# Values token-major with 512 weight columns at once, the last 16 tokens in float32 on four column groups, and gates inside the attention heads

## The chip, the cores and the metric

The kernel runs on one core of one Trainium2 chip. The metric is the device time of one execution in microseconds (us); three runs of the kernel before gave 1594.56 to 1595.37 us with a median of 1594.84 us. One of its executions was taken by the hardware profiler, and every row below comes from that one. PE is the matrix engine, PEld its loading of the operand that stays in the array, ACT, DVE and POOL are the scalar, vector and general engines, SP issues most of the transfers.

## The reference

The reference is one transformer layer in float32 over 512 tokens with 16 learned tokens ahead of them (T = 528), width 1024: a gated feed-forward block, a mixer, a second feed-forward block and a last norm. Only the mixer matters here:

```python
proj = u @ w_in                       # u = rmsnorm(h); columns are split into
# rq rk (4 heads x 256), rv rg (4 x 512), aq ak av (8 x 128), iq ik iw, g_ret, g_att
yr = retention(rope(rq), rope(rk), rv)    # 4 heads, values 512 wide
yr = (silu(rg) * yr) @ w_ret_out
ya = dsa_attention(rope(aq), rope(ak), av, rope(iq), rope(ik), iw) @ w_att_out
merged = sigmoid(g_ret) * yr + sigmoid(g_att) * ya
return merged @ w_mix_out
```

In both branches a weight matrix over pairs of tokens (decayed q·k in retention, a softmax over selected keys in attention) is multiplied with the values `rv` or `av`. The keys that attention selects come from an index score, made from `iq`, `ik` and `iw`, of which the 128 best per token are kept.

## The kernel before

Activations lie with features on the 128 partitions and tokens along the free dimension. Every float32 factor is split into two parts of the type fp32r: `hi` is a rounded copy made by ACT (L117), `lo` the rest made by DVE (L118). `mm3` (L152) then makes three matmuls for each of the 8 blocks of 128 input features: hi·hi, lo·hi, hi·lo. A weight tile of 128 output columns is the stationary operand and the tokens stream past it, 512 of them in one matmul, or all 528 in two of 264. So one projection of 128 columns is 24 matmuls of 512 or 48 of 264 columns. Weights come by transfers of up to 1 MB into two buffers (`raw`), and their split parts go into three buffers each (`whi`, `wlo`).

The order of PE's instructions is the order of the program text (PE is under `manual_schedule`). The other engines' instructions are put in order by a scheduler that works by dependencies and program order. Background work, the index scores (`index_steps`) and the choice of the keys (`select_steps`), is cut into steps that the program calls for between projections with `step()`.

The mixer goes like this:

1. Index projections: `psiq` four times, `psik` once; then rotary embedding on ACT, DVE and POOL, which yields `iw` (L593), `ikh` (L599) and `ikl` (L600), the operands of the index scores `psw` (L606) and `pssc` (L617). The scores' two matmuls of a pair use 64 rows of the array each.
2. Retention, four heads. For each head: query (`psrq`, twice) and key (`psrk`, twice), each pair turned by `rope_pair` (DVE L688, POOL L691, then the split into `rkh` and `rkl`); the output projection of the head before (`ret_out`, `psro`); then four blocks of 128 value columns. For each block stand: `gated()`, the gate's projection `psrg`; `values()`, the value projection `psrv` over all 528 tokens; in the first block `decayed()`, the decayed scores `psst` (L751); `weigh()` of the block before, `pspv` (L771, tail L772); and `by_token()`, in which PE turns the block's values so that tokens lie on the partitions: four transposes of 128x128 (L788) and one for the last 16 tokens (L789), whose results ACT and DVE split. In the first head the gate and the value projection of the first block stand between the key projection and `decayed()`, and index steps are held back until the key projection.
3. Attention, eight heads: `psaq`, `psak`, `psav`, scores `psS` (L936), softmax, transposes of the probabilities `psPT` (L952), `psao` (L771), and the same `by_token()` (L788, L789). While one head's softmax runs, PE makes the next head's projections. Six of the eight `g_ret` gates (`psgate`) come in the last head and after it.
4. After the heads: the eight `g_att` gates (`psga`), the output projection of attention (`psat`), the last projection of the mixer (`psmo`).

The second feed-forward block's down projection (`psd`, L1143) already has the other layout: 128 tokens of the hidden activations are stationary, and 512 columns of weights stream, four blocks of tokens for each piece of weights of four feature blocks.

Of the kernel before, what the change touches and what calls it, by code (L numbers as in the profile page):

```python
# [18 lines left out]
P = 128  # L19
D = 1024  # L20
# [61 lines left out]
def kernel(ctx: ExitStack, tc: tile.TileContext, x, meta, g1, wg1, wu1, wd1, gm,  # L82
# [113 lines left out]

    def rstd_steps(ssum, n, dim, dst, sp, psum):


        ends = [min(b * P, n - P) for b in range(-(-n // P))]  # L200
        nb = len(ends)
        col = psum()
        for b, t0 in enumerate(ends):
            nc.tensor.matmul(col[:, b : b + 1], ssum[:, t0 : t0 + P], ones, start=True, stop=True)
        yield from rstd_of(col, n, dim, dst, sp, psum, P - (n - S))

    def rstd_of(col, n, dim, dst, sp, psum, tail):
# [4 lines left out]
        r = sp.tile([P, 5], F32, tag="rcol", name="rcol", bufs=2)  # L212
# [39 lines left out]

    gap(cpool, 8)


    with pool("f1") as fp, pool("gps", 2, PSUM) as gps, ExitStack() as later:
# [205 lines left out]
        for f0, nf in ((0, 12), (12, 10)):  # L462
# [38 lines left out]
            for c in range(0, KD, 2):  # L501
# [7 lines left out]
                for i in range(2):  # L509
                    k = c + i  # L510
                    nc.vector.scalar_tensor_tensor(hT[k], halves(pss[i])[1], 0.5, hT[k], ALU.mult, ALU.add)
                    if f0:
                        h, l = new_x(k, XO)
                        split_gain(hT[k], gains[:, 1, k : k + 1], h, l)
                        add_square(hT[k], ssum2, k == 0, fp, bufs=4)
                        nc.scalar.dma_start(hd[k], hT[k][:, REAL])
# [48 lines left out]
    with pool("ixt") as ixt:  # L565
        tp.update(pool=ixt, bufs=8)
        norm = rstd_steps(ssum2, T, D, R2, ixt, lambda: mm_tile("psn"))
        pss = []
        cols = Cols(w_in, OFF_IQ, 4)
        for i in range(4):  # L570
# [4 lines left out]
            if i < 3:  # L575
                next(norm)
        cos, sin = rope_tables(0, ixt)
        iq = []
# [68 lines left out]
    def tails(p, n):  # L647

        tp.update(v=[stacked(p, f"vtail{i}", P) for i in range(2)], p=stacked(p, "ptail", n), turn=0)

# [26 lines left out]
    with pool("rt") as rt:  # L677
        tp.update(pool=rt, bufs=7)
        cos, sin = rope_tables(2, rt)
        gap(rt, 48)  # L680
# [84 lines left out]
        def weighted(ps, vb, prob):  # L765

            for kb in range(4):
                vh, vl = vb[0][:, kb, :], vb[1][:, kb, :]
                ph, pl = prob[kb]
                for i, (a, b) in enumerate(((vh, ph), (vh, pl), (vl, ph))):  # L770
                    nc.tensor.matmul(ps[:, KQ[kb] :], a, b, start=kb == 0 and i == 0, stop=False)  # L771
            nc.tensor.matmul(ps[:, KQ[4] :], vb[2][:TR], tp["p"][:TR, :NM], start=False, stop=True)  # L772

        def weigh(c, vb, sg, prob, ssum, o):
# [4 lines left out]
            nc.vector.tensor_tensor(t[:, :S], ps, sg, ALU.mult)  # L779
            oh = rt.tile([P, S], F32R, tag=f"oh{c}", name="oh")  # L780
            ol = rt.tile([P, S], F32R, tag=f"ol{c}", name="ol")
            split(t[:, :S], oh, ol)
            o.append((oh, ol))

        def by_token(vt, vp):
            ps = mm_tile("psvt").rearrange("p (a b) -> p a b", a=2)
            for kb in range(4):
                nc.tensor.transpose(ps[:, 0, kb * P : (kb + 1) * P], vt[:, kb * P : (kb + 1) * P], ident)  # L788
            nc.tensor.transpose(ps[:NM, 1, 0:P], vt[:, 4 * P : T], ident)  # L789
            vh = vp.tile([P, 4, P], F32R, tag="vh", name="vh", bufs=2)  # L790
            vl = vp.tile([P, 4, P], F32R, tag="vl", name="vl", bufs=2)
            split(ps[:, 0, :].rearrange("p (b c) -> p b c", b=4), vh, vl)
            tail = tp["v"][tp["turn"]]
            tp["turn"] ^= 1
            split_rows(ps[:NM, 1, 0:P], tail, "hhl")
            return vh, vl, tail

        bg = [index_steps()]
        last_weigh = last_norm = last_out = None
        for h in range(RH + 1):  # L800
# [20 lines left out]
            cols = Cols(w_in, OFF_RK + h * DK, 2)  # L821
            if h == 0:
                bg[0] = steps
            ka = proj_all(cols, "psrk")
# [13 lines left out]
            ssum = rt.tile([P, S], F32, tag="ossum", name="ossum", bufs=2)  # L838
            cv = Cols(w_in, OFF_RV + h * DV, 4)
            cg = Cols(w_in, OFF_RG + h * DV, 4)  # L840
# [9 lines left out]

            def values():
                ps = proj_all(cv, "psrv")
                vt = tmp()
                ins = nc.vector.tensor_tensor(vt, ps, R, ALU.mult)
                step(ins)
                return vt

            for c in range(4):
                if c == 0:
                    sg = gated()  # L860
                    vt = values()
                    prob = decayed(rq, rk, u)
                else:
                    vt = values()
                    sg = gated()
                    weigh(*pend, prob, ssum, o)
                if h == 0:
                    step()
                    step()
                pend = (c, by_token(vt, rt), sg)  # L870
            rn = rt.tile([P, S], F32, tag="rn", name="rn")
# [7 lines left out]


    with pool("ao") as ao:
        ao_parts = []
        with pool("at") as at:
# [10 lines left out]
            tails(at, 48)  # L894
            cq, ck, cv = (Cols(w_in, o_, AH, step=1) for o_ in (OFF_AQ, OFF_AK, OFF_AV))
            scale = DH**-0.5
# [18 lines left out]

            def proj_v():
                w = cv.next()
                parts, ps = halves(mm_tile("psav"))
                mm3(parts, w, xs, KD)
                vt = tmp()  # L920
                nc.vector.tensor_tensor(vt, ps, R, ALU.mult)
                return vt

# [38 lines left out]

            def weigh_v(parts, v):
                ps = sm_tile("psao")
                weighted(ps, v, parts)
                oh = ao.tile([P, S], F32R, tag=f"ah{len(ao_parts)}", name="ah")
                ol = ao.tile([P, S], F32R, tag=f"al{len(ao_parts)}", name="al")
                split(ps, oh, ol)
                ao_parts.append((oh, ol))

            q, k, vt = proj_q(), proj_k(), proj_v()
            for h in range(AH):
                more = h + 1 < AH
                scores(q, k)
                if h == 0:
                    v = by_token(vt, at)
                if more:
                    q, k = proj_q(), proj_k()
                else:
                    for c in (2, 3, 4):  # L980
                        gate_acc(c, gate(gr, at, wide=True))
                parts = transpose_p()
                if more:
                    vt = proj_v()
                else:
                    gate_acc(5, gate(gr, at, wide=True))
                weigh_v(parts, v)
                if more:
                    v = by_token(vt, at)

# [4 lines left out]
        with pool("ou") as ou:  # L995
            tp.update(pool=ou, bufs=3)
            for c in (6, 7):
                gate_acc(c, gate(gr, ou))
            cols = Cols(w_in, OFF_GA, KD)
            sa = []  # L1000
            for c in range(KD):
                w = cols.next()
                ps = sm_tile("psga")
                mm3([(ps, REAL)], w, xs, KD)
                t = ou.tile([P, S], F32, tag=f"sa{c}", name="sa")
                nc.vector.tensor_tensor(t, ps, Rr, ALU.mult)
                nc.scalar.activation(t, t, AF.Sigmoid)
                sa.append(t)
            cols = Cols(w_ao, 0, KD)
# [14 lines left out]
    with pool("om") as ou:  # L1024
# [36 lines left out]
        for _ in norm:  # L1061
            pass
    mgs.close()
    accs.close()
    sel.close()
# [116 lines left out]
```

## Time and profile before

| quantity | value |
|---|---|
| median of three runs | 1594.84 us (1594.56 to 1595.37) |
| profiled execution | 1595.39 us |
| its span (first to last instruction) | 1593.5 us |
| PE busy | 1582.4 us in 9731 matmul records |
| DVE busy | 820.9 us |
| ACT busy | 570.6 us |
| POOL busy | 232.7 us |

The page's first part gives the busy time of each engine, the second the busy tenths in 40 slices of the span, the fourth the chain of work that ended last. In the timeline view each row has the start, the length, the engine, the line, the operation, what it writes and reads, and how many instructions of the same kind are merged in it; a row of PE begins with the shape of the stationary operand (rows*columns). Matmuls overlap, so their lengths don't add up: what one costs is the distance from its start to the next start.

### The profile page before, as it was taken

What the parts mean: (1) busy time and instruction counts of PE and PEld (TensorE: products, weight loads), DVE (VectorE), ACT (ScalarE), POOL (GpSimd) and SP (SyncE); (2) the same over time, 40 slices, a digit from 0 to 9 for tenths busy, and PEclk for the clock granted to TensorE, in tenths of its full rate; (3) what the DMA queues carried; (4) which work ended last, traced back from release to release, by engine and by line L of the source; (5) the groups of instructions that cost most, each with busy time, mean ns of one, the idle gap of its engine ahead of it and who ended that gap; (6) DMA issues with size and microseconds to landing.
All of it is one profiled execution on the core that took longest, in us unless ns stands there. A gap on an engine that the chain in (4) does not pass through costs nothing.

```text
span 1593.5 us, 23010 instructions
## 1 busy us (share of the span) xinstructions
PE 1582.4 (99%) x9731; PEld 1421.5 (89%) x9731; DVE 820.9 (52%) x1263; ACT 570.6 (36%) x912; POOL 232.7 (15%) x187
## 2 busy tenths in 40 slices
PE   9999999999999999999999999999999999999998
PEld 8999999999888898899898999988888888888886
DVE  5443234334575776866845666753454434324434
ACT  6322222233544333233333555553234323223223
POOL 1211001111320200301304210011002111001100
PEclk9999999999999999999999999999999999999999
DMA  5222232224332132231312322313243322232222
GB/s 185 90 84 83 93 113 80 97 80 143 108 112 67 42 116 78 80 116 40 119 54 72 112 69 66 94 58 103 80 138 101 118 96 89 89 113 90 93 91 81
DMA packets 148582, 148.66 MB, mean 93 GB/s; under 512 B 3288, under 2 KB 137456, under 8 KB 148480
## 3 DMA queue, kind: packets, MB, share of 16 engines
q1 hardware_dynamic: 143872, 138.16, 26.9%
q10 hardware_dynamic: 4544, 9.03, 1.7%
q8 instruction: 76, 1.25, 0.3%
q14 instruction: 26, 0.21, 0.0%
q0 software_dynamic: 64, 0.01, 0.0%
HBM read 143.00 MB, written 4.19 MB: 92 GB/s over the span
## 4 chain that ended last, share of the span: by engine, by line
PE 91%; DVE 4%; ACT 2%; issue 1%; POOL 1%; DMA 1%; ACTq 0%; POOLq 0%; DVEq 0%
PE psu L152 15%; PE psg L152 15%; PE psd L152 8%; PE psd L1143 7%; PE psrv L152 6%; PE psrg L152 6%; PE psrk L152 3%; PE psgate L152 3%; PE psmo L152 3%; PE psat L152 3%; PE psga L152 3%; PE psak L152 3%; PE psav L152 3%; PE psrq L152 2%; PE psro L152 2%; PE psaq L152 2%
## 5 line engine op out<-in xcount | busy, mean ns | idle before, releaser
L117 ACT ACTIVATE whi<-raw 128x1024 fp32r<-128x1024 f32 (+3 forms) x284 | 277.7, 979 | 841.8 <-PE psu L152 165.6
L118 DVE TENSOR_TENSOR wlo<-raw,whi 128x1024 fp32r<-128x1024 f32 (+3 forms) x284 | 338.6, 1192 | 179.0 <-ACT whi L117 175.3
L152 PE MATMUL psu<-xl,whi 128*128 128x264 f32 (+1 forms) x528 | 141.0, 319 | 0.0
L152 PE MATMUL psu<-xh,whi 128*128 128x264 f32 (+1 forms) x528 | 140.6, 318 | 0.0
L152 PE MATMUL psu<-xh,wlo 128*128 128x264 f32 (+1 forms) x528 | 140.6, 318 | 0.0
L152 PE MATMUL psg<-xl,whi 128*128 128x264 f32 (+1 forms) x496 | 133.3, 321 | 0.0
L152 PE MATMUL psg<-xh,wlo 128*128 128x264 f32 (+1 forms) x496 | 132.8, 321 | 0.0
L152 PE MATMUL psg<-xh,whi 128*128 128x264 f32 (+1 forms) x496 | 132.8, 320 | 0.0
L152 PEld LDWEIGHTS psu<-xh,wlo 128*128 128x128 f32 x528 | 88.1, 188 | 6.9
L152 PEld LDWEIGHTS psu<-xh,whi 128*128 128x128 f32 x528 | 87.8, 188 | 6.8
L152 PEld LDWEIGHTS psu<-xl,whi 128*128 128x128 f32 x528 | 87.4, 188 | 6.9
L152 PEld LDWEIGHTS psg<-xh,wlo 128*128 128x128 f32 x496 | 82.6, 188 | 6.9
L152 PEld LDWEIGHTS psg<-xh,whi 128*128 128x128 f32 x496 | 82.3, 188 | 6.7
L152 PEld LDWEIGHTS psg<-xl,whi 128*128 128x128 f32 x496 | 82.0, 188 | 6.8
L483 POOL TENSOR_TENSOR t<-t,R 128x528 f32<-128x528 f32 x22 | 37.5, 1707 | 262.3 <-ACT t L482 262.3
L1118 POOL TENSOR_TENSOR t<-t,R 128x512 f32<-128x512 f32 x22 | 38.4, 1748 | 251.6 <-ACT t L1117 251.6
L152 PE MATMUL psd<-hl,whi 128*128 128x264 f32 x352 | 71.3, 284 | 0.0
L152 PE MATMUL psd<-hh,wlo 128*128 128x264 f32 x352 | 70.8, 283 | 0.0
L152 PE MATMUL psd<-hh,whi 128*128 128x264 f32 x352 | 70.6, 282 | 0.0
L1143 PE MATMUL psd<-whi,hh 128*128 128x512 f32 x176 | 68.5, 389 | 0.0
L1143 PE MATMUL psd<-wlo,hh 128*128 128x512 f32 x176 | 68.5, 389 | 0.0
L1143 PE MATMUL psd<-whi,hl 128*128 128x512 f32 x176 | 68.5, 389 | 0.0
(316 smaller groups left out, 3555.8 us busy)
## 6 DMA issues: line engine op xcount, KB each, us to landing
raw<-in_w_in_dram SPq DMA_DIRECT2D x34, 1024.0 KB, 4.9
raw<-in_ffn_w_up_dram SPq DMA_DIRECT2D x22, 1024.0 KB, 5.0
raw<-in_ffn_w_gate_dram SPq DMA_DIRECT2D x21, 1024.0 KB, 5.0
raw<-in_w_in_dram SPq DMA_DIRECT2D x25, 512.0 KB, 3.5
raw<-in_ffn_w_down_dram SPq DMA_DIRECT2D x10, 1024.0 KB, 4.8
raw<-in_w_ret_out_dram SPq DMA_DIRECT2D x16, 512.0 KB, 3.4
raw<-in_ffn_w_down_dram SPq DMA_DIRECT2D x8, 768.0 KB, 4.3
raw<-in_ffn_w_down_dram SPq DMA_DIRECT2D x8, 640.0 KB, 3.9
```

The lines of the kernel that those rows point to most:

```text
L117: nc.scalar.activation(hi, src, AF.Copy)
L118: eng.tensor_tensor(lo, src, hi.bitcast(F32), ALU.subtract)
L152: nc.tensor.matmul(o, a[:, k, :], b[:, sl], start=first and k == 0 and i == 0, stop=last and k == nk - 1 and i == 2)
L483: nc.gpsimd.tensor_tensor(t, t, R, ALU.mult)
L1118: nc.gpsimd.tensor_tensor(t, t, R, ALU.mult)
L1143: nc.tensor.matmul(pss[b], a[:, bs], m[:, k % 2, :], start=k0 + k == 0 and i == 0, stop=k0 + k == nf - 1 and i == 2)
```

## The change

The values are now made token-major. `values(c0, parts, meanwhile)` takes 512 columns of weights in two pieces of four feature blocks (1 MB each). For each of four blocks of 128 tokens the tokens' activations are stationary and the 512 weight columns stream, so that the result already has tokens on the partitions; `split_gain` scales it by the token's norm factor (kept per token in `rtok`) and splits it. The five transposes of every block of 128 columns and their multiply are gone. One call replaces four `values()` and `by_token()` of a retention head, or of four attention heads: six calls in all. The last 16 tokens don't fill a block; they are multiplied in plain float32 out of the unsplit weights, with the activations of 16 tokens (`xlast`, scaled by POOL) stationary, 128 weight columns streaming, and the four groups of 128 weight columns written to partitions 0, 32, 64 and 96 of one PSUM tile `psvl`. `place()` splits those rows into four tiles `vtail`.

The order changes with it. In the first retention head `values` stands before the query projection and calls a background step after each block of tokens; the index steps are no longer held back. In the later heads it stands after `ret_out`. `decayed()` follows directly after it (in the first head: directly after the key projection), and the four gates follow, each but the first with a `weigh()` behind it. In attention two calls (before the first head's scores, and in the fourth head) replace `proj_v` of each head; in its place in the other heads stands one gate: six of `g_ret`, and in the last head three of `g_att`.

```diff
+    def values(c0, parts, meanwhile=lambda: None):
+        two = [mm_tile("psv") for _ in range(2)]
+        ps = [two[b // 2][:, b % 2 * S : (b % 2 + 1) * S] for b in range(4)]
+        rest = sm_tile("psvl")
+        for k0 in (0, 4):
+            raw = load_w(w_in[k0 * P : (k0 + 4) * P, c0 : c0 + 4 * P], 4, 4 * P)
+            w_at[0] = XO
+            ws = [split_w(raw[:, i : i + 2, :]) for i in (0, 2)]
+            w_at[0] = 0
+            for k in range(k0, k0 + 4):
+                for c in range(4):
+                    nc.tensor.matmul(rest[32 * c : 32 * c + NM, :P], xlast[:, k, :], raw[:, k - k0, c * P : (c + 1) * P],
+                                     start=k == 0, stop=k == KD - 1)
+            for b in range(4):
+                bs = slice(b * P, (b + 1) * P)
+                for k in range(4):
+                    (xh, xl), (wh, wl) = xs(k0 + k), ws[k // 2]
+                    for i, (a, m) in enumerate(((xh, wh), (xl, wh), (xh, wl))):
+                        nc.tensor.matmul(ps[b], a[:, bs], m[:, k % 2, :], start=k0 + k == 0 and i == 0,
+                                         stop=k0 + k == KD - 1 and i == 2)
+                if k0:
+                    split_gain(ps[b].rearrange("p (c d) -> p c d", c=4), rtok[:, b : b + 1],
+                               parts[0][:, :, bs], parts[1][:, :, bs])
+                meanwhile()
...
-        def by_token(vt, vp):
-            ps = mm_tile("psvt").rearrange("p (a b) -> p a b", a=2)
-            for kb in range(4):
-                nc.tensor.transpose(ps[:, 0, kb * P : (kb + 1) * P], vt[:, kb * P : (kb + 1) * P], ident)
-            nc.tensor.transpose(ps[:NM, 1, 0:P], vt[:, 4 * P : T], ident)
...
+            if h == 0:
+                place = values(OFF_RV, parts, step)
             cols = Cols(w_in, OFF_RQ + h * DK, 2)
-            if h == 0:
-                steps, bg[0] = bg[0], iter(())
...
+            if h:
+                place = values(OFF_RV + h * DV, parts, step)
+            prob = decayed(rq, rk, u)
+            vs = place()
...
             for c in range(4):
-                if c == 0:
-                    sg = gated()
-                    vt = values()
-                    prob = decayed(rq, rk, u)
-                else:
-                    vt = values()
-                    sg = gated()
+                sg = gated()
+                if c:
                     weigh(*pend, prob, ssum, o)
...
-                parts = transpose_p()
-                if more:
-                    vt = proj_v()
+                pt = transpose_p()
+                if h == 3:
+                    place = half_values(1)
+                elif more:
+                    wide_gate()
                 else:
-                    gate_acc(5, gate(gr, at, wide=True))
-                weigh_v(parts, v)
-                if more:
-                    v = by_token(vt, at)
+                    wide_gate_a()
+                weigh_v(h, pt, vs[h])
+                if h == 3:
+                    vs += place()
```

More of the change, by code (lines that the diff above doesn't have):

```diff
@@ L566 @@
         tp.update(pool=ixt, bufs=8)
-        norm = rstd_steps(ssum2, T, D, R2, ixt, lambda: mm_tile("psn"))
+        norm = rstd_steps(ssum2, T, D, R2, ixt, lambda: mm_tile("psn"), rtok)
         pss = []
@@ L647, in tails, with place @@
     def tails(p, n):
-        tp.update(v=[stacked(p, f"vtail{i}", P) for i in range(2)], p=stacked(p, "ptail", n), turn=0)
+        tp.update(v=[stacked(p, f"vtail{i}", P) for i in range(4)], p=stacked(p, "ptail", n))
+    def values(c0, parts, meanwhile=lambda: None):
[22 more added lines that the diff above has]
+                meanwhile()
+        def place():
+            for c in range(4):
+                rows = slice(32 * c, 32 * c + NM)
+                split_rows(rest[rows, :P], tp["v"][c], "hhl")
+            return [(parts[0][:, c, :], parts[1][:, c, :], tp["v"][c][:TR]) for c in range(4)]
+        return place
     def split_rows(src, t, order):
@@ L678 @@
         tp.update(pool=rt, bufs=7)
+        parts = [rt.tile([P, 4, S], F32R, tag=f"vo{i}", name="vo") for i in range(2)]
         cos, sin = rope_tables(2, rt)
@@ L767, in weighted @@
             for kb in range(4):
-                vh, vl = vb[0][:, kb, :], vb[1][:, kb, :]
+                vh, vl = (part[:, kb * P : (kb + 1) * P] for part in vb[:2])
                 ph, pl = prob[kb]
@@ L878, with gate_a @@
             gate_acc(c, t)
+    sas = ExitStack()
+    sap = sas.enter_context(pool("sap", 1, side="right"))
+    gr = Cols(w_in, OFF_GR + 2 * P, KD - 2, step=1)
+    ga = Cols(w_in, OFF_GA, KD, step=1)
+    sa = []
+    def gate_a(ps, gp):
+        mm3([(ps, REAL)], ga.next(), xs, KD)
+        t = gp.tile([P, S], F32, tag=f"sa{len(sa)}", name="sa")
+        nc.vector.tensor_tensor(t, ps, Rr, ALU.mult)
+        nc.scalar.activation(t, t, AF.Sigmoid)
+        sa.append(t)
     with pool("ao") as ao:
-        ao_parts = []
+        vo = [ao.tile([P, AH, S], F32R, tag=f"vo{i}", name="vo") for i in range(2)]
+        ao_parts = [(vo[0][:, c, :], vo[1][:, c, :]) for c in range(AH)]
         with pool("at") as at:
@@ L914, in proj_k, with half_values @@
                 return k
[L916 to L922, printed above, removed]
+            def half_values(i):
+                return values(OFF_AV + i * 4 * P, [v[:, 4 * i : 4 * i + 4, :] for v in vo])
             def scores(q, k):
@@ L996 @@
             tp.update(pool=ou, bufs=3)
[L997 to L1008, printed above, removed]
+            while len(sa) < KD:
+                gate_a(sm_tile("psga"), ou)
             cols = Cols(w_ao, 0, KD)
```

61 lines of the change are left out of this document (26 added, 35 removed).

## The prediction

> **What bounds the kernel now.** I read the page's busy shares first, then its chain, then PE's timeline around one value block.
>
> ```profile
> PE 1582.4 (99%) x9731; PEld 1421.5 (89%) x9731; DVE 820.9 (52%) x1263; ACT 570.6 (36%) x912; POOL 232.7 (15%) x187
> PE   9999999999999999999999999999999999999998
> PE 91%; DVE 4%; ACT 2%; issue 1%; POOL 1%; DMA 1%; ACTq 0%; POOLq 0%; DVEq 0%
> ```
>
> PE is busy in every slice and is 91% of the chain; the others have room on average. So the change is worth what it takes from PE's row of starts, less what it adds there, plus the time PE newly waits. Times are distances between starts. One block of retention:
>
> ```profile
> 800.94 0.40 PE L152 MATMUL psrg<-xh,whi 128*128 128x512 f32 x1
> ...
> 806.42 0.39 PE L771 MATMUL pspv<-ph,vh 128*128 128x512 f32 x1
> ...
> 808.41 0.64 PE L788 MATMUL psvt<-ident,tmp 128*128 128x128 f32 x4
> 808.89 0.27 PE L789 MATMUL psvt<-ident,tmp 128*16 128x128 f32 x1
> 808.92 0.49 PE L152 MATMUL psrv<-xh,whi 128*128 128x264 f32 x2
> 809.25 0.40 PE L152 MATMUL psrv<-xl,whi 128*128 128x264 f32 x2
> 809.49 0.40 PE L152 MATMUL psrv<-xh,wlo 128*128 128x264 f32 x2
> ...
> 814.77 0.40 PE L152 MATMUL psrg<-xh,whi 128*128 128x512 f32 x1
> ```
>
> The reader sees work without a pause: 24 matmuls of 512 columns in 5.48 us (806.42 - 800.94; 0.228 each), five transposes in 0.51, 48 matmuls of 264 in 5.85 (0.12 each).
>
> **The change part by part.** *Values and transposes removed.* 814.77 - 808.41 = 6.36 us per block. Attention's blocks are the same, 0.51 and 5.85:
>
> ```profile
> 905.46 0.49 PE L152 MATMUL psav<-xh,whi 128*128 128x264 f32 x2
> ...
> 911.31 0.40 PE L771 MATMUL psao<-pth,vh 128*128 128x512 f32 x1
> ...
> 913.33 0.65 PE L788 MATMUL psvt<-ident,tmp 128*128 128x128 f32 x4
> 913.84 0.37 PE L936 MATMUL psS<-ak,aq 128*128 128x264 f32 x1
> ```
>
> Four heads of four blocks and eight of one make 24: 152.6 us.
>
> *The 512 tokens added.* Six calls of 2 pieces x 4 token blocks x 12 matmuls are 576 of 512 columns. I take the gate's 0.228: 131.5 us. That weights stream and tokens stand costs nothing: `psd` runs so, in the same pieces and buffers, with no idle time.
>
> ```profile
> L1143 PE MATMUL psd<-whi,hh 128*128 128x512 f32 x176 | 68.5, 389 | 0.0
> ```
>
> Bounds by single distances in rows further down: 0.22 from `psik` to `psrq`, 0.23 within `pssc`, so 126.7 to 132.5. Net with the gate's price -21.1 us, 0.88 per block.
>
> *The last 16 tokens added.* 192 plain float32 matmuls (6 x 2 x 16), which the trace of before has in no such shape. Three things bound them:
>
> ```profile
> 904.23 1.36 PE L952 MATMUL psPT<-ident,pj 128*128 128x128 f32 x11
> 905.43 0.27 PE L954 MATMUL psPT<-ident,pj 128*16 128x128 f32 x1
> L204 PE MATMUL psn<-ones,ossum x32: 164/250/250, 529.9 to 853.1; 128*128 128x1 f32 x32
> 443.72 0.35 PE L606 MATMUL psw<-ident,iw 8*128 8x8 f32 x3
> 443.99 0.50 PE L617 MATMUL pssc<-ikh,iqh 64*128 64x512 f32 x2
> 444.33 0.40 PE L617 MATMUL pssc<-ikl,iqh 64*128 64x512 f32 x2
> 444.56 0.39 PE L617 MATMUL pssc<-ikh,iql 64*128 64x512 f32 x2
> 444.89 0.51 PE L152 MATMUL psrk<-xh,whi 128*128 128x264 f32 x2
> 445.24 0.41 PE L152 MATMUL psrk<-xl,whi 128*128 128x264 f32 x2
> ```
>
> 128 float32 columns take 0.109 (11 transposes in 1.20 us); with only 16 columns standing still 0.12 (after the tail at 808.89 the first pair took 0.03 + 0.33 instead of 0.24). A plain float32 matmul is two instructions: `psn` has 32 records where the code issues 16. So one costs 0.218 alone, 41.9 us for all. But matmuls on different groups of the array run side by side: two of `pssc` take 0.23 where two of 512 columns would take 0.46. Starts keep the program's order, and both passes of one matmul need the same group; so I expect a chain: the second pass of a group beside the first of the next, 0.109 per matmul, 20.9 us. All four groups at once would be a quarter of 41.9, 10.5. Entering and leaving the grouped form costs 0.3: the three pairs last 0.90 instead of 0.69, and the next pair 0.35 instead of 0.24. Twelve such trips: 3.6. Sum 24.5, ends 14.1 and 45.5. I take the middle because order and groups are what the rows show.
>
> *Index steps no longer held back.* In the first head PE goes from `psik` to the first half of `psvl`, 12 matmuls, then `psw` and `pssc`. Their operands come late:
>
> ```profile
> 426.31 0.39 PE L152 MATMUL psik<-xh,wlo 128*128 128x512 f32 x1
> 426.53 0.39 PE L152 MATMUL psrq<-xh,whi 128*128 128x512 f32 x1
> 433.21 1.22 DVE L118 TENSOR_TENSOR wlo<-raw,whi 128x1024 fp32r<-128x1024 f32 x1
> 435.13 0.69 DVE L593 TENSOR_TENSOR iw<-psik,R 8x512 f32<-8x512 f32 x1
> 437.28 0.63 ACT L599 ACTIVATE ikh<-tmp 64x512 fp32r<-64x512 f32 x1
> 437.29 1.38 DVE L600 TENSOR_TENSOR ikl<-tmp,ikh 64x512 fp32r<-64x512 f32 x2 [0.76 <-ACT ikh L599]
> ```
>
> Before, 17 us of `psrq` and `psrk` lay over this. After, DVE and ACT have the same chain (rotary embedding, two weight splits, `iw`, `ikh`, `ikl`) in the same order, so `ikl` is there at 438.67 and the pairs end near 439.2. From 426.53 that is 12.7 us, in which PE has 2.0 (half of `psvl`: 1.74 + 0.3) + 2.7 + 1.2 (443.72 to 444.89) = 5.9: a wait of 6.7. With `psvl` at its ends 5.0 to 7.6. PE takes its instructions in program order, so all its later work queues behind; the weights for the next piece are split meanwhile and don't come later than PE.
>
> *`decayed()` directly behind the key projection, first head.* Before, `psrg` and `psrv` (11.3 us) hid the key's rotary embedding:
>
> ```profile
> 450.77 0.40 PE L152 MATMUL psrg<-xh,whi 128*128 128x512 f32 x1
> 452.38 0.70 DVE L688 TENSOR_TENSOR tmp<-psrk,cos 128x528 f32<-128x528 f32 x1
> 453.00 0.70 DVE L688 TENSOR_TENSOR tmp<-psrk,sin 128x528 f32<-128x528 f32 x1
> 453.23 3.06 POOL L691 TENSOR_TENSOR tmp<-tmp 128x528 f32<-128x528 f32 x2 [5.53 <-DVE tmp L688]
> 454.58 0.65 ACT L117 ACTIVATE rkh<-tmp 128x528 fp32r<-128x528 f32 x1 [2.31 <-POOL tmp L691]
> ```
>
> After, PE has nothing between. The key projection ends where `psrg` starts, at 450.77. The products with its first half are now made while the second half is projected; then one product 0.70, two POOL operations 3.06, one split 0.65 are 4.4, with hand-overs 4.7, and the third matmul waits 0.3 more for `rkl`: 5.0. Lower end 4.4; upper 6.1, with both of the first half's products (0.62 apart each in DVE's row) late too. Heads two to four have `ret_out` and `values` in between: nothing.
>
> *Waits that go.* The page shows few: `psrg` waited 0.8 for weights behind `ret_out`, where `psvl`, which needs no split, now stands; and 0.5 goes with the earlier index steps. -1.3 (0 to -3).
>
> ```profile
> L152 PE MATMUL psrg<-xh,wlo 128*128 128x512 f32 x128 | 50.1, 392 | 0.8 <-DVE wlo L118 0.8
> L152 PE MATMUL psrq<-xh,whi 128*128 128x512 f32 x64 | 25.5, 399 | 0.5 <-ACT tmp L620 0.5
> ```
>
> *At nothing:* the gates in the heads: PE makes the same 16, one gate (5.48) lies where `psav` (5.85) lay and covers the same softmax; their activation alternates with the softmax's, whose table then has to be loaded anew in each head, on an ACT that is 36% busy. If that cover failed, 1.3 us a head. DVE and ACT lose the multiply and keep the splits. SP's transfers stay at 1 MB, two buffers; `psvl` reads `raw` first in each piece, so it is free early. POOL's nine small operations lie beside PE.
>
> *Sum:* -21.1 + 24.5 + 6.7 + 5.0 - 1.3 = +13.8. The profiled execution took 1595.4 (its span 1593.5), 0.55 over the median; from the median 1594.8 the forecast is 1608.6 us. Its own range, by the ends of the 512-column price (-4.8, +1.0), the wait at `decayed()` (-0.6, +1.1) and the waits that go (-1.7, +1.3), is 1602 to 1612.
>
> *A rule that speaks against the change.* The Trainium skill, "TensorE: Matmul & The Clock Gate", Part 1, says that PE idle for a window of about 3.4 us falls back to half its clock for as long. By it, an estimate, the wait of 5.0 would cost up to 1.7 us more. Here only the start bears on it: the first ten matmuls of 512 columns took 4.63, about twice the 0.228 apiece of later ones; no later pause of that length exists in the trace of before, so it doesn't show the fall.
>
> ```profile
> 1.46 4.63 PE L318 MATMUL psg<-idle 128*128 128x512 f32 x10 [1.46 <-DVE idle L286]
> ```
>
> **The rivals.** *No overlap of groups:* each of 192 matmuls takes its two passes alone, 45.5 for `psvl`, and the first wait shrinks to 5.0: -21.1 + 45.5 + 5.0 + 5.0 - 1.3 = +33.1, 1627.9. For it: no row shows float32 passes in groups. Against: `pssc`.
>
> *Four groups at once:* 14.1, the wait grows to 7.6: +4.3, 1599.1. For it: `pssc` starts pairs together. Against: the second pass stands between one group's first and the next group's. The Trainium skill, same page, Part 3, measured three column groups at 2.38 times the speed and later groups 4 ns apart; that would favour this case, and no run here shows column groups.
>
> *Faster:* the four groups' two passes share one 0.109 slot (48 x 0.109 = 5.2) and entering the form hides behind `psv`: -21.1 + 5.2 + 8.0 + 5.0 - 1.3 = -4.2, 1590.6. It decides where half a `psvl` costs under 0.8 us in all. Against: `psn`'s two records, and `pssc`'s 0.3.
>
> **How the numbers follow.** Chain 0.48, no overlap 0.20, four at once 0.17, faster 0.15. The range takes the rivals in from 1593 to 1629; left out are most of the fastest case and a tenth of the slowest. About 0.2% is what this measurement can tell, 3.2 us. Four at once lies at +0.27%, and with a wait 1 us shorter within the bound, so it is shared: slower 0.73, same 0.12, faster 0.15.
>
> **What would show it.** Right: `psv` starts 0.228 apart; 16 `psvl` matmuls in about 1.8 us; PE idle some 6 us around the first `psw` and `pssc`, released by DVE and ACT, and 5 us before the first `psst`, released by ACT `rkh`. Wrong: 16 `psvl` in 0.9 or 3.5; `ikl` or `rkh` ready earlier against the psik and psrk ends; new idle time before `psPT` from the tables, or before `psv` from weights split late.

## The result, and the profile after

The changed kernel takes 1639.56 us (median of four runs, 1638.59 to 1640.06) against 1595.11 us for the kernel before beside it: 1.0277 times, with a 95% interval of 1.0264 to 1.0291. It is 44.5 us slower. The forecast was 1608.6 us with a range to 1629: the direction was right, the size was a third of what came, and the time lies outside the range.

The profiled execution took 1638.59 us, its span 1636.7, 43.2 us more than before; all rows below come from it unless another kernel is named. Lines of the changed file: weights are split at L117 and L118 as before, `psv` is L678, `psvl` L671, the gain and split of a token block ACT L121 and DVE L122 (`vo`), `psst` L796, `pssc` L624. First the page's busy times, PE's slices, its granted clock and the shares of the chain:

```profile
PE 1591.6 (97%) x9419; PEld 1394.0 (85%) x9419; DVE 812.7 (50%) x1239; ACT 588.9 (36%) x924; POOL 238.1 (15%) x199
PE   9999999999898989989999999899999999999998
PEclk9999999999899999999999999999999999999999
PE 89%; DVE 6%; ACT 2%; issue 1%; POOL 1%; ACTq 0%; POOLq 0%; DVEq 0%
```

PE now has five slices below nine tenths beside the last one, where before only the last one was; one slice has a lower clock; and DVE stands on the chain with 6% instead of 4%. PE's busy time rose by 9 us with 312 fewer records, though at their undisturbed rate the new matmuls need 10 us less than the old (the account below): many run longer than they should. The same by stage. In the view by windows the columns are the stretch, its length, PE's busy time and records, and the granted clock. The first row of each kernel reaches from the end of `psik` to the first `psgate` (retention), the second from there to the first `psmo` (attention). Before:

```profile
426.53:836.56 410.03, 407.84 (x2517) 1.00 0.26 83
836.56:1178.52 341.96, 341.84 (x2035) 1.00 0.27 84
```

After:

```profile
426.06:870.51 444.45, 417.44 (x2309) 0.97 0.23 76
870.51:1221.94 351.43, 341.87 (x1931) 1.00 0.27 81
```

Retention lost 34.4 us and attention 9.5, which is all of it. In retention 27 us are idle time (444.45 - 417.44, against 2.2 before), and the granted clock of 0.97 there is four stretches at half the clock, 27.3 us together. The list of PE's waits (what waited for whom: us in total, times, longest) names them:

```profile
PE psv L678 <- DVE vo L122: 21.6, 12, 4.2
PE psst L796 <- ACT rkh L117: 4.5, 1, 4.5
PE psv L678 <- DVE wlo L118: 2.9, 2, 1.6
PE psvl L671 <- DVE ptl L118: 2.0, 1, 2.0
PE psv L678 <- ACT whi L117: 1.8, 1, 1.8
...
PE psaq L152 <- DVE stat L970: 1.1, 5, 0.2
PE psw L613 <- DVE iw L600: 1.0, 1, 1.0
PE pssc L624 <- ACT ikh L606: 1.0, 1, 1.0
```

Of these the forecast had the second, and as one wait of the index steps the last two; the `whi` wait and 1.3 of the `wlo` one stand at the same place. The largest, 21.6 us in twelve waits, two for each call of `values`, it did not have. The twelve stand ahead of the second and the fourth token block of a call's second piece. Here is one of the longest in PE's timeline, and then DVE's rows just before its end:

```profile
599.08 0.39 PE L678 MATMUL psv<-wlo,xh 128*128 128x512 f32 x1
603.71 0.79 PE L678 MATMUL psv<-whi,xh 128*128 128x512 f32 x1 [4.25 <-DVE vo L122]
604.30 0.63 PE L678 MATMUL psv<-whi,xl 128*128 128x512 f32 x1
604.73 0.63 PE L678 MATMUL psv<-wlo,xh 128*128 128x512 f32 x1
```

```profile
601.06 0.69 DVE L641 MATCH_REPLACE8 score<-top,score 128x512 f32<-128x512 f32 x1
601.66 1.22 DVE L118 TENSOR_TENSOR wlo<-raw,whi 128x1024 fp32r<-128x1024 f32 x1
602.91 0.75 DVE L122 SCALAR_TENSOR_TENSOR vo<-psv,rtok,vo 128x512 fp32r<-128x512 f32 x1
```

At 599.08 PE has finished token block 0 of the call. PSUM is where PE's results lie until another engine reads them. Block 1 shares a PSUM tile with block 0 (`ps = two[b // 2]`: two tiles of 1024 columns, two blocks in each), and PE may not write into that tile before DVE has read block 0 out of it, which ends at 603.66. Block 0's reading stands on DVE behind steps of the selection and a weight split. The rows that follow the pause also start 0.43 us apart instead of 0.23.

That leaves the terms that came out as hoped. Sixteen `psvl` matmuls, 32 records:

```profile
426.15 1.07 PE L671 MATMUL psvl<-raw,xlast 128*16 128x128 f32 x32
427.15 0.50 PE L678 MATMUL psv<-whi,xh 128*128 128x512 f32 x1
```

They take 1.00 us, so the twelve halves take 12.0. Undisturbed `psv` matmuls start 0.227 apart, and 576 of them are 130.6 us.

Over the whole span the account is (distances from start to next start, summed by the tile that is written): out go `psrv` 93.7, `psav` 46.7, `psvt` 12.3; in come `psv` 169.9 (39.3 more than its 130.6) and `psvl` 12.0; `psrk` and `psst` are 6.5 longer, `pssc` and `psw` 4.3, `psPT` 2.3, `psS` 1.4, the rest 0.3 shorter. The sum is +43.4.

### The profile page after: what moved, and what is told of

The parts are those of the page before. It is cut to its first block, busy times and chain, and to the rows that moved or that the text cites. A ratio compares the mean times of both kernels' runs of the same rounds, so it can differ in the third digit from the quotient of the medians.

```text
span 1636.7 us, 22474 instructions
## 1 busy us (share of the span) xinstructions
PE 1591.6 (97%) x9419; PEld 1394.0 (85%) x9419; DVE 812.7 (50%) x1239; ACT 588.9 (36%) x924; POOL 238.1 (15%) x199
## 4 chain that ended last, share of the span: by engine, by line
PE 89%; DVE 6%; ACT 2%; issue 1%; POOL 1%; ACTq 0%; POOLq 0%; DVEq 0%
PE psu L152 15%; PE psg L152 14%; PE psd L152 8%; PE psv L678 7%; PE psd L1170 7%; PE psrg L152 5%; PE psrk L152 3%; PE psak L152 3%; PE psaq L152 3%; PE psrq L152 3%; PE psgate L152 3%; PE psmo L152 3%; PE psro L152 3%; PE psga L152 3%; PE psat L152 3%; PE pspv L816 2%
## 5 line engine op out<-in xcount | busy, mean ns | idle before, releaser
L117 ACT ACTIVATE whi<-raw 128x1024 fp32r<-128x1024 f32 (+3 forms) x284 | 278.0, 980 | 834.2 <-PE psu L152 165.6
L118 DVE TENSOR_TENSOR wlo<-raw,whi 128x1024 fp32r<-128x1024 f32 (+3 forms) x284 | 338.8, 1194 | 218.2 <-ACT whi L117 214.2
L678 PE MATMUL psv<-whi,xh 128*128 128x512 f32 x192 | 80.6, 420 | 23.4 <-DVE vo L122 21.6
L678 PE MATMUL psv<-wlo,xh 128*128 128x512 f32 x192 | 77.7, 405 | 2.9 <-DVE wlo L118 2.9
L152 PE MATMUL psro<-vo,whi 128*128 128x512 f32 x256 | 79.0, 390 | 0.0
L678 PE MATMUL psv<-whi,xl 128*128 128x512 f32 x192 | 77.2, 402 | 0.0
L678 PEld LDWEIGHTS psv<-whi,xh 128*128 128x128 f32 x192 | 37.6, 196 | 39.5 <-DVE vo L122 26.6
```

The source lines that it names most:

```text
L117: nc.scalar.activation(hi, src, AF.Copy)
L118: eng.tensor_tensor(lo, src, hi.bitcast(F32), ALU.subtract)
L152: nc.tensor.matmul(o, a[:, k, :], b[:, sl], start=first and k == 0 and i == 0, stop=last and k == nk - 1 and i == 2)
L678: nc.tensor.matmul(ps[b], a[:, bs], m[:, k % 2, :], start=k0 + k == 0 and i == 0, stop=k0 + k == KD - 1 and i == 2)
```

## The experiments

The theory was formed on those rows: (a) the shared tile makes PE wait for each block's reading; (b) pauses of PE cost more than their length, since matmuls behind them run at half their rate; (c) the two pauses of the first head come from the order alone. The rivals were that DVE is late whatever the tile, and that the slow rows have a cause of their own.

**Token blocks dealt to the two tiles in turn.**

```diff
-        ps = [two[b // 2][:, b % 2 * S : (b % 2 + 1) * S] for b in range(4)]
+        ps = [two[b % 2][:, b // 2 * S : (b // 2 + 1) * S] for b in range(4)]
```

> The four token blocks of a call are dealt to the two PSUM tiles in turn (blocks 0 and 2 in one, 1 and 3 in the other) instead of two after each other into the same tile. Theory 'shared tile': PE's idle time before psv that DVE's vo releases (21.6 us in the changed kernel) comes from a block that may not write into a tile while the block before it is still being read from it; then it falls to under 6 us (what is left where the selection's steps hold up DVE), and with the half-clock stretches that follow the longest pauses some 18 to 26 us go: 1614 to 1622 us. Rival 'DVE is late anyway': the reading of one block is slower than PE's next block, so the wait only moves by one block: no change, 1636 to 1641.

Measured: 1614.07 us, 1.0115 [1.0099, 1.0131] times the kernel before; 25.5 us of the 44.5 are gone by one index. The list of waits of this kernel has, in place of the 21.6:

```profile
PE psv L678 <- DVE vo L122: 1.9, 2, 1.5
```

So 19.7 us were the sharing of tiles; of the other 5.8, slow rows of `psv` are 2.7 (6.5 to 3.8 us; the granted clock is half for 17.1 us inside this kernel instead of 27.3), and the rest, restarts behind the waits among it, was not taken apart. DVE was not too slow: a block is read while the next one, in the other tile, is made.

**Index steps held back in the first head, as before the change.**

```diff
+                steps, bg[0] = bg[0], iter(())
                 place = values(OFF_RV, parts, step)
...
             cols = Cols(w_in, OFF_RK + h * DK, 2)
+            if h == 0:
+                bg[0] = steps
             ka = proj_all(cols, "psrk")
```

> In the first head the steps of the index are held back until the key projection, as in the kernel before. Theory 'pause then slow clock': the waits around the first psw and pssc (5.1 us together) go, and so does the stretch in which matmuls of 512 columns start 0.427 us apart instead of 0.227 around them: -7 to -10 us, 1629.5 to 1632.5. Rival 'pause only': -5 us, 1634.5, with the 0.427 stretch still there. Rival 'the wait only moves to the values of the first head or to decayed': 0 to -2 us.

Measured: 1641.35 us (1639.52 to 1643.28), 1.0287 [1.0270, 1.0303]: no gain; the nearest expectation is the last, with a lead that lasted longer. The waits on `iw` and `ikh` are gone, but the list of waits has the ones on the values' own weights still (1.8 for `whi`), and new ones:

```profile
PE psv L678 <- DVE vo L122: 22.6, 12, 3.5
...
PE pssc L624 <- ACT tmp L627: 1.1, 1, 1.1
PE psro L152 <- ACT tmp L627: 0.8, 1, 0.8
```

Counted from the end of `psik`, the first `psrq` of the four heads starts after 33.4, 103.8, 222.1 and 336.7 us, in the changed kernel after 40.3, 109.4, 222.9 and 336.4. The lead of 6.9 us is partly work put off, and it is gone by the third head: steps not taken during the first head's values are left over, the program runs off what remains in one go ahead of the second head's `ret_out`, and there PE waits for ACT to empty the score tiles; behind these waits the granted clock is half from 563.64 to 567.05. So the pause at the first `psw` is real, but holding the steps back is no remedy as long as the values stand ahead of the query.

**The decayed scores behind the first gate.**

```diff
-            prob = decayed(rq, rk, u)
-            vs = place()
...
                 sg = gated()
+                if c == 0:
+                    prob = decayed(rq, rk, u)
+                    vs = place()
```

> In each retention head the decayed scores and the placing of the last 16 tokens stand behind the first gate's matmuls instead of ahead of them. Theory: the 4.5 us of idle time before the first psst of head one goes, and with it the stretch behind it in which matmuls start 0.427 us apart (about 2.2 us): -6 to -7.5 us, 1632 to 1633.5. Without a clock effect: -4.5 us, 1635. Rival: the first gate then needs weights that are not split yet, and the pause moves to psrg: 0 to -2 us.

Measured: 1632.29 us, 1.0230 [1.0214, 1.0246]: -7.3 us, as expected with the slow rows. The wait on `rkh` is gone from the list, `psrg` got no new one (`pssc` got two of 0.4), and the scores start 0.23 apart.

**Work in place of the pause.** Does the pause make the rows behind it slow? This kernel makes 19 more matmuls, whose result nobody reads, where PE waited for `rkh` in the first head.

```diff
+            if h == 0:
+                pb = sm_tile("pskb")
+                for _ in range(19):
+                    nc.tensor.matmul(pb, xs(0)[0][:, :P], xs(0)[0][:, :S], start=True, stop=True)
             prob = decayed(rq, rk, u)
```

> The changed kernel with 19 more matmuls of 512 columns into a PSUM tile that nobody reads, ahead of the first psst of head one: 4.3 us of work (19 x 0.227) where PE now idles 4.5 us. Theory 'a pause costs its own length and then a stretch at half the clock': the wait is filled, the next psst and psrg start 0.227 us apart instead of 0.427, and the time falls by 2 to 3 us although PE makes more: 1636.5 to 1637.5. Rival 'no clock effect, the 0.427 comes from something else there (operands, reads of PSUM)': the time stays, 1639 to 1640, and the 0.427 stretch stays.

Measured: 1637.90 us, 1.0265 [1.0250, 1.0280]. With 4.3 us more of work it is 1.7 us below the changed kernel, less than expected, and the two intervals overlap; by the time alone nothing would be decided. The rows decide, and the granted clock over them, which the view by windows has in its column behind PE's records. The changed kernel at this place:

```profile
495.34 0.79 PE L796 MATMUL psst<-rqh,rkh 128*128 128x512 f32 x1 [4.49 <-ACT rkh L117]
...
496.96 0.63 PE L796 MATMUL psst<-rqh,rkh 128*128 128x512 f32 x1
497.39 0.63 PE L796 MATMUL psst<-rql,rkh 128*128 128x512 f32 x1
...
500.24 0.41 PE L796 MATMUL psst<-rqh,rkh 128*128 128x272 f32 x1
```

```profile
495.34:500.24 4.90, 4.90 (x12) 0.50 0.00 0
```

And with the pause filled:

```profile
491.98 4.50 PE L873 MATMUL pskb<-xh 128*128 128x512 f32 x19
496.69 0.50 PE L796 MATMUL psst<-rqh,rkh 128*128 128x512 f32 x1 [0.21 <-ACT rkh L117]
...
498.05 0.39 PE L796 MATMUL psst<-rqh,rkh 128*128 128x512 f32 x1
498.28 0.39 PE L796 MATMUL psst<-rql,rkh 128*128 128x512 f32 x1
...
499.84 0.29 PE L796 MATMUL psst<-rqh,rkh 128*128 128x272 f32 x1
```

```profile
496.69:499.84 3.15, 2.86 (x13) 1.00 0.00 0
```

The same matmuls with the same operands start 0.43 us apart behind the pause and 0.23 without it, and the granted clock is 0.50 and 1.00. From the first `psst` to the first of 272 columns it is 4.90 us against 3.15; the twelve matmuls between take 2.5 at full rate (six at 0.23, six at 0.18), so this pause cost 2.4 us beyond its length, of which 1.75 went with the filling; the filled kernel still restarts, and waits 0.29 for `rkl`. The Trainium skill, "TensorE: Matmul & The Clock Gate", Part 1, has half the clock after an idle window and 426.7 ns between matmuls of 512 columns in that state; the distances agree.

**The last 16 tokens on one column group.** What do the four groups give?

```diff
-                    nc.tensor.matmul(rest[32 * c : 32 * c + NM, :P], xlast[:, k, :], raw[:, k - k0, c * P : (c + 1) * P],
-                                     start=k == 0, stop=k == KD - 1)
+                    nc.tensor.matmul(rest[:NM, c * P : (c + 1) * P], xlast[:, k, :], raw[:, k - k0, c * P : (c + 1) * P],
+                                     start=k == 0 and c == 0, stop=k == KD - 1 and c == 3)
...
-                rows = slice(32 * c, 32 * c + NM)
-                split_rows(rest[rows, :P], tp["v"][c], "hhl")
+                split_rows(rest[:NM, c * P : (c + 1) * P], tp["v"][c], "hhl")
```

> All 192 float32 matmuls of the last 16 tokens on one column group of the array (rows 0 to 15 of the tile, four column ranges) instead of on four. Theory 'four groups at once' (32 passes in 1.0 us): alone they take 0.109 us a pass, 3.5 us per half call, 2.5 us more in each of the twelve, +30 us less what the waits give back (up to 6): 1663 to 1670 us. Theory 'chain' (one group's second pass beside the next group's first): 1.7 us more in each, +20: 1660. Theory 'no overlap': no change, 1639.

Measured: 1659.87 us, 1.0414 [1.0394, 1.0434]: +20.3. The number is the one that the chain gave, and would mislead; its rows are those of the first theory:

```profile
425.75 3.67 PE L671 MATMUL psvl<-raw,xlast 128*16 128x128 f32 x32
429.35 0.50 PE L678 MATMUL psv<-whi,xh 128*128 128x512 f32 x1
```

A half takes 3.60 us instead of 1.00, and twelve halves 31 more. Waits gave 5.3 back (PE's idle time inside the span falls from 36.9 to 31.6) and the slow stretches of `psv` 4.1 (6.5 to 2.4 us); another 1.5 stays open.

**Both remedies together.** The first and the third edit at once.

> Token blocks dealt to the two PSUM tiles in turn, and the decayed scores behind the first gate. Apart they gave -25.5 and -7.3 us. If they are independent: 1614.1 - 7.3 = 1606.8 us. If the second only shifted DVE's work into the place that the first had relieved: 1610 to 1614.

Measured: 1606.12 us, 1.0067 [1.0052, 1.0082]: the two gains add up, to 0.7 us.

**The first head like the others.** With the tiles dealt in turn, its values stand behind the key projection as in the heads that follow, and the index steps are held back as in the kernel before; the decayed scores stay behind the values.

```diff
-            if h == 0:
-                place = values(OFF_RV, parts, step)
             cols = Cols(w_in, OFF_RQ + h * DK, 2)
+            if h == 0:
+                steps, bg[0] = bg[0], iter(())
...
             cols = Cols(w_in, OFF_RK + h * DK, 2)
+            if h == 0:
+                bg[0] = steps
...
-            if h:
-                place = values(OFF_RV + h * DV, parts, step)
+            place = values(OFF_RV + h * DV, parts, step)
             prob = decayed(rq, rk, u)
```

> Token blocks dealt in turn, and head one of retention like the others: its values behind its key projection (where they lie over the key's rotary embedding, ahead of the decayed scores), and the index steps held back until the key projection as in the kernel before. Theory 'both pauses of head one come from the order alone': the 5.1 us around the first psw and pssc, the 4.5 before the first psst and the half-clock stretches behind them (some 6) go: 1614.1 - 15 = 1599, range 1597 to 1602. Rival 'given back', as when the index steps alone were held back (the first head won 6.1 us and the next one and a half lost them again, as the leftover steps were run off in one go): 1605 to 1610.

Measured: 1599.40 us, 1.0025 [1.0016, 1.0035]: -14.7 against the kernel with the tiles alone. Waits on `iw`, `ikh`, `whi` and `rkh` are gone, and no `psv` or `psst` starts 0.43 behind the one before it any more. Here the held-back steps are taken in the first head's values, and nothing is given back.

**The last 16 tokens one block later, in attention's second call.** In the fourth head `psvl` took a small PSUM tile that DVE (`ptl`) still read. On the kernel just shown:

```diff
             for b in range(4):
+                if b == late:
+                    if rest is None:
+                        rest = sm_tile("psvl")
+                    for k in range(k0, k0 + 4):
+                        for c in range(4):
+                            nc.tensor.matmul(rest[32 * c : 32 * c + NM, :P], xlast[:, k, :], raw[:, k - k0, c * P : (c + 1) * P],
+                                             start=k == 0, stop=k == KD - 1)
```

`late` is 1 in attention's second call and 0 in the others; the same matmuls ahead of the loop go.

> As the kernel with head one like the others, and in the second value call of attention the matmuls of the last 16 tokens stand behind the first token block instead of ahead of it, so that they don't wait for the PSUM slot that the split of the last transposed probabilities (ptl) still reads. Theory: the idle 2.0 us at that place and the stretch of eight matmuls at 0.427 behind it go: -3 to -3.7 us against that kernel, 1594 to 1598. Rival 'psv then waits there': no change against it.

Measured: 1596.14 us, 1.0004 [0.9995, 1.0013]: -3.3, as expected, and no different from the kernel before. The profiled executions differ by 2.1 (1598.74 and 1596.63), the wait alone: in the profile of the kernel with `psvl` ahead of the loop there are no slow rows behind it, against what I had expected from another kernel's. Other executions have some: a window at half the clock (3.41 us, see the last section) takes 0.001 off the granted clock of an execution, which is 0.999 in the profiled one, but 0.998 or 0.997 in eight of this kernel's ten, and 0.999 or more in all ten with `psvl` one block later.

**`psao` in the large tiles.** One line on the last kernel: `ps = mm_tile("psao")[:, :S]` for `sm_tile("psao")`.

> As the last kernel (token blocks dealt in turn, head one like the others, the last 16 tokens behind the first token block in attention's second call), and psao of attention in the ring of large PSUM tiles instead of the small ones, where psaq of the next head got its slot. Theory: five waits of 0.225 us between psS and psaq go: -1.1 us, 1595.0. Rival: the large ring then holds up psv or psak: no change or +1 to +3.

Measured: 1595.27 us, 0.9997 [0.9988, 1.0006]. A step of 0.9 us that the intervals don't resolve. The next kernel, which has this edit too, shows that the waits of `psaq` are gone and that `psS` waits 1.0 instead, on `vo`.

**Fewer selection steps during the values.** On that kernel, in heads two to four:

```diff
-                meanwhile()
+                if not k0 or every:
+                    meanwhile()
...
-            place = values(OFF_RV + h * DV, parts, step)
+            place = values(OFF_RV + h * DV, parts, step, every=h == 0)
...
-                if h == 0:
-                    step()
-                    step()
+                step()
+                if h == 0:
+                    step()
```

> As that, and in heads two to four the selection's steps are taken in the first piece of a value call alone, with one more behind each gate, so that the gain of the token blocks (DVE vo) does not queue behind them. Theory: the waits of 1.5 and 0.4 us on vo in the second pieces go: -1.5 to -2 us against it, 1593 to 1594, a little below the kernel before (1595.5). Rival: the steps hold up DVE behind the gates instead, or the ones left over run off in one go ahead of attention: 0 to +5 us.

Measured: 1592.70 us, 0.9980 [0.9971, 0.9989]: -2.6 us, and below the kernel before by 2.9. PE is busy for 1575.6 us, 99% of the span. Its four longest waits:

```profile
PE psv L681 <- DVE wlo L118: 1.6, 1, 1.6
PE psg L323 <- DVE idle L291: 1.5, 1, 1.5
PE psS L970 <- DVE vo L122: 1.0, 1, 1.0
PE psv L681 <- DVE tmp L555: 0.8, 1, 0.8
```

No wait of `psv` on `vo` is left. The change keeps its layout and its four groups here; only tiles and order differ. It is worth those 2.9 us once most of the waits are out: 0.2%, with an interval of 0.1 to 0.3%, and no more than the 3.2 us that the prediction called the least that this measurement can tell.

## Why the prediction was wrong

Point by point, by its own steps:

- *Values and transposes removed, 152.6.* Right: 152.7 (93.7 + 46.7 + 12.3).
- *The 512 tokens added, 131.5.* The matmuls themselves are right, 130.6. The sentence beside it is the step that failed: "That weights stream and tokens stand costs nothing: `psd` runs so, in the same pieces and buffers, with no idle time." The pieces and buffers of the weights are the same. The PSUM tiles are not: `psd` has one for each of its four token blocks (`pss = [bank("psd") for _ in range(4)]`); `psv` has two for four blocks. I compared what flows in and not where the results go. That put 21.6 us of waits into the kernel, and 19.7 of them went when the blocks were dealt otherwise. Both facts were there beforehand, in the line of the diff that cuts the tiles and in the gain that DVE makes from each block.
- *DVE and ACT keep the splits, at nothing.* Wrong in the same place: DVE's average of 52% hid that a token block's reading can stand behind selection steps (which makes a wait of 4.25 us where most of the twelve are 1.56).
- *The last 16 tokens, 24.5.* Too high. 12.0, plus 0.1 to enter and 0.1 to leave in each of twelve trips, is 14.4, near the forecast's lower end of 14.1. The chain of second passes does not exist: the rival "four groups at once", to which I gave 0.17, was right about `psvl`, and its time of 1599.1 was still 40 us off, because of the step above.
- *Index steps, a wait of 6.7.* The place was right, the releasers in part: `whi`, `wlo`, `iw` and `ikh` are 5.1 us in all, but 3.1 of them stand ahead of `psv`, on weights split late, which the forecast had put at nothing ("don't come later than PE") and named as a sign of being wrong; and the second token block starts 13.75 us after the end of `psik` where the forecast gave 12.7 to the scores' end. Less 4.9 of work (1.0 for `psvl`, 2.7, 1.2) that is 8.8 lost: above the forecast's upper end of 7.6 for this `psvl`, because rows between the pauses run slow (the granted clock is half from 432.23 to 442.47).
- *`decayed()`, a wait of 5.0.* Right: 4.5, released by `rkh`. The rule on the clock was priced at up to 1.7 and kept out of the sum; it cost 2.4 here, because the clock was half for 6.83 us (493.67 to 500.50) and not for one window. This is the second thing mis-sized: the sum took pauses at their length.
- *Waits that go, -1.3.* About right: the 0.8 of `psrg` on `wlo` and the 0.5 of `psrq` are gone, as is one of 0.5 of `psst` that was not named; but `psrg` now waits 0.7 for ACT to empty score tiles (`tmp`, L627): 1.1 in all. The time per projection is the same.
- *Gates at nothing.* Right for their matmuls; `psaq` waits 1.1, less than the 1.3 a head that was named as the price of a lost cover, and from another cause (a PSUM slot).
- Not foreseen at all: `psvl` behind `ptl` in attention's fourth head, 2.0 us in its row, 3.3 by its experiment.

From +13.8 to +43.2: 21.6 for the tiles; 2.0 for the slot, 1.6 for one late weight split, 1.1 for `psaq`; some 10.4 for rows at half rate (6.5 in `psv`, 2.4 in `psst`, the rest around the first `pssc`; by the granted clock 11.2, half of the 22.4 us that PE was busy in the four stretches); -0.9 for the cheaper bulk, -12.5 for `psvl`, -2.1 for the idle time of the two foreseen waits, which was shorter than put. That is 21.2 of 29.4. Of the remaining 8.2, 7.0 lie in `psv` (39.3 - 25.8 of idle time, its end at `psw` included, - 6.5): starts behind a pause or a change of form, each 0.1 to 0.2 late, which the forecast had only for `psvl`.

The range failed with the sum. Its two ends were made from the price of `psvl` alone; no rival had the values themselves waiting for their readers.

## What to carry to other kernels

When a pattern of matmuls is taken over from another place of the kernel, compare where its results go as closely as where its operands come from: which PSUM tile each group of matmuls writes, who reads that tile last, and what else that engine has queued. Two results in one tile are one resource; give neighbours in time different tiles. Price a pause of PE by its length and by what the clock does behind it: here one of 4.5 us cost 2.4 us more, and work in its place was cheaper than the pause. In these traces the clock fell behind windows of 3.41 us in which PE was busy for less than half; two shorter pauses in one window can do it too, as the 1.1 and 0.8 us did with the index steps held back.

## What was not expected of the hardware

Sixteen-row float32 matmuls on four column groups ran 3.6 times as fast as on one (1.00 against 3.60 us for 32 records), though each matmul is two records. The Trainium skill, "TensorE: Matmul & The Clock Gate", Part 3, gives 2.38 for three groups; the runs agree with its direction and have no three.

The slow state does not begin with the pause's end. After a wait of 3.13 us two matmuls still start 0.34 and 0.24 us apart, then eight 0.43 or a little less, and then it is over. The rows, and the granted clock by windows:

```profile
718.41 0.50 PE L678 MATMUL psv<-whi,xh 128*128 128x512 f32 x1 [3.13 <-DVE vo L122]
718.75 0.44 PE L678 MATMUL psv<-whi,xl 128*128 128x512 f32 x1
718.99 0.63 PE L678 MATMUL psv<-wlo,xh 128*128 128x512 f32 x1
```

```profile
715.54:718.95 3.41, 0.54 (x2) 1.00 0.83 286
718.95:722.37 3.42, 3.42 (x9) 0.50 0.00 0
```

So it depends on more than the pause. In the ten profiles (the changed kernel and nine of the experiments), behind 445 us, all six pauses of 4.2 to 4.6 us have rows at 0.43 within the next 7 us, five of six of 3.1 to 3.6 us, five of twelve of 1.8 to 2.2 us, and none of 52 of 1.45 to 1.75 us.

The granted clock shows on what. In these traces it changes only on a grid of 3.41 us that runs through the whole kernel: inside the kernel the stretches at half the clock last 3.41, 6.83, 10.24 or 13.65 us, and the two windows above are two of the grid. In these ten profiles and that of the kernel before, up to PE's last matmul, the clock fell to half behind 24 windows, and PE was busy for at most 46% of each; of the some 5100 other windows at full clock, one was busy for 45% and all others for 47% or more. So the same pause can go either way, by how the grid divides it. Here is the one ahead of `psvl` in attention with the tiles dealt in turn, whole in one window:

```profile
1009.18 1.07 PE L671 MATMUL psvl<-raw,xlast 128*16 128x128 f32 x32 [2.01 <-DVE ptl L118]
```

```profile
1006.72:1010.13 3.41, 1.40 (x37) 1.00 0.01 2
1010.13:1013.54 3.41, 3.41 (x13) 0.50 0.58 159
```

And in the kernel whose first head is like the others, divided between two:

```profile
995.38 1.07 PE L671 MATMUL psvl<-raw,xlast 128*16 128x128 f32 x32 [2.02 <-DVE ptl L118]
```

```profile
990.56:993.97 3.41, 2.81 (x25) 1.00 0.03 5
993.97:997.39 3.42, 2.01 (x36) 1.00 0.00 0
997.39:1000.80 3.41, 3.41 (x16) 1.00 0.56 154
```

The Trainium skill, same page, Part 1, says that the window is 3.4 us long and runs freely, and the grid agrees; that a window must be idle for the clock to fall does not, since only two of the 24 were idle throughout. Matmuls of 16 columns count as work: with the last 16 tokens on one column group a window held nothing else (32 records), and the clock was full in it and in the next one (816.98 to 820.40).

```profile
813.57:816.98 3.41, 3.41 (x32) 1.00 0.00 0
```

This is read off the traces as they are: no pause was varied in length or moved on the grid by itself, and why one window at 45% kept its clock stays open.
